# Sharing the 512-column work tiles of the gate and up products between two pools, by pairs

## The chip, the cores and the metric

The kernel runs on one core of one Trainium2 chip. The metric is device time in microseconds of the whole program: the time before is 2663.41 us, the median of 3 runs (2663.13 to 2663.88).

## The reference

One encoder layer on x of shape (1, 2048, 1024): RMSNorm, a projection, windowed attention beside a bidirectional state-space branch, a gated merge with a residual, and then the feed-forward part, which is the one that the change touches:

```python
x = x + (jax.nn.silu(h2 @ w_ffn_gate[layer]) * (h2 @ w_ffn_up[layer])) @ w_ffn_down[layer]
return rmsnorm(x, norm_f_g)
```

Here h2 is the normalised x (2048 x 1024), and the gate and up matrices are 1024 x 2816.

## The kernel before

Three phases follow each other. `phase3` (L1267) ends with the feed-forward part: `gate_up` twice, once for each half of the 2048 tokens, and then `down`. Precision is kept by splitting each operand into a high and a low float32r part (`hi_lo`, L1002: ScalarE copies the high part, VectorE subtracts the low part) and multiplying high*high, high*low and low*high (`PASSES`).

**The unit of work.** A matrix product of 2 x 2 blocks is done with seven block products instead of eight (a Strassen-Winograd scheme; the products are named 11, S2, S1, 12, S3, S4, 22 in `BLK`). `w_unit` (L1034) loads a 1024 x 256 slice of the gate or the up matrix into two raw tiles, forms the sums of its blocks on GpSimd (`sums`, L1021, into a tile T of which there is one) and splits the seven into high and low weights. `h_blocks` (L1006) does the same for the activations of one half of the tokens: 14 tiles H, loaded once for each half. `gu_unit` (L1060) is one unit: seven products of 12 matmuls each, accumulated in three PSUM tiles A, B and C, with the outputs taken out of PSUM between products:

- c1 copies A after product 11 (L1071, ScalarE); u2 = B + c1 after S2 (L1075, VectorE); c5 copies C after S1 (L1079, ScalarE); u3 = B + c1 after S3 (L1086, VectorE); u2 += C after S4 (L1089); c1 += B after 22 (L1095); u3 += c5 (L1093, GpSimd).
- Products accumulate on the same PSUM tile. S3 cannot start on B before u2 has been taken out of it, 22 not before u3, and S4 not on C before c5.

**The pair.** A gate unit and an up unit of the same 256 columns make a pair; 11 pairs make up each half. `pair_up` (L1123) joins them: the gate's four results become Z["11"] (a new tile sg, written by the Silu from PSUM), Z["12"] (u2), Z["22"] (u3) and Z["21"] (c1), and the up unit's results are multiplied into them (L1134). So a gate's c1, u2, u3 and sg live until `z_blocks` (L1098) has read them: it forms two sums zsum and two more in place on GpSimd (L1114 to L1119), splits each of the seven blocks and stores them for `down`. An up unit's c1, u2 and u3 and every c5 live only until they have been added or multiplied in.

**The two pools.** All of these are tiles of 128 x 512 float32 from `t_tile` (L1054): eight buffers in the pool `tq`, six in the pool `tp`. Before the change, the gate's c1, u2, sg and u3 and the up's c1, u2 and u3, seven tiles in a pair, come from the pool of six; the two c5 and the two zsum come from the pool of eight. The first pair of the first half differs (`first`), since the pool of six does not exist yet when it begins: its c1 and u2 are in the pool of eight and its c5 in the pool of six.

**What sets the order.** `gate_up` (L1138) goes through the pairs: gate, weights of the next gate, up, then `z_blocks`; the first and the last pair of a half run their gate and up alternately, product by product (L1145 to L1147). In the first half `h_sums_later` (L991) runs after the second, fourth, sixth and eighth pair: GpSimd makes sums for the second half's activations in the tile T and stores them. After the last pair of the first half the 14 tiles H are filled anew. Each engine executes its instructions in a fixed order. The framework's scheduler writes that order when the kernel is built (`schedule_with_timeline_sim`, L1347), going forward in time through a simulation: an instruction that comes earlier in the program goes first if it is ready, and a new tile gets a buffer when one is free. So with another supply of buffers the order can change from the first affected tile on, and not before it.

Of the kernel before, what the change touches and what calls it, by code (L numbers as in the profile page):

```python
# [86 lines left out]
def rest(gen):  # L87
    for _ in gen:
        pass


class Kern:
# [7 lines left out]
    def load(self, out, in_):  # L100
        self.nc.sync.dma_start(out=out, in_=in_)  # L101
# [955 lines left out]
            return self.tq.tile([128, 512], F32, tag="t", name=name, bufs=8)  # L1057
        return self.tp.tile([128, 512], F32, tag="t", name=name, bufs=6)

    def gu_unit(self, W, H, fin, first=False):  # L1060

        s, v, p = self.s, self.v, self.p
        tl = self.t_tile

        def prod(ps, n, first, last):
            self.chain(ps, [(W[n][:, a, k], H[n][k // 2][:, b, k % 2]) for k in range(4) for a, b in PASSES], first, last)

        A, B, C = self.ps("pj"), self.ps("b"), self.ps("a")
        prod(A, "11", True, False)
        c1 = tl(first, "c1")  # L1070
        s.activation(c1, A, AF.Copy)  # L1071
        yield
        prod(B, "S2", True, False)
        u2 = tl(first, "u2")
        v.tensor_tensor(u2, B, c1, ADD)  # L1075
        yield
        prod(C, "S1", True, False)
        c5 = tl(not first, "c5")
        s.activation(c5, C, AF.Copy)  # L1079
        yield  # L1080
        prod(A, "12", False, True)
        fin("11", A)
        yield
        prod(B, "S3", False, False)
        u3 = tl(False, "u3")
        v.tensor_tensor(u3, B, c1, ADD)  # L1086
        yield
        prod(C, "S4", False, True)
        v.tensor_tensor(u2, C, u2, ADD)  # L1089
        fin("12", u2)  # L1090
        yield
        prod(B, "22", False, True)
        p.tensor_tensor(u3, u3, c5, ADD)  # L1093
        fin("22", u3)
        v.tensor_tensor(c1, B, c1, ADD)  # L1095
        fin("21", c1)
# [23 lines left out]
        put("S3", Z["21"])  # L1120
        put("S4", Z["12"])

    def pair_up(self, W, Wu, H, first=False):  # L1123

        s, v, p = self.s, self.v, self.p
        Z = {}

        def gate(n, z):
            g = self.t_tile(False, "sg") if n == "11" else z
            s.activation(g, z, AF.Silu)  # L1130
            Z[n] = g

        def up(n, z):
            (p if n == "22" else v).tensor_tensor(Z[n], Z[n], z, MULT)  # L1134

        return Z, self.gu_unit(W, H, gate, first), self.gu_unit(Wu, H, up, first)

    def gate_up(self, units, W, hh, H, nxt, bg, after=None, head=None):  # L1138


        n = len(units)
        load = lambda u: self.w_unit(*units[u]) if u < n else nxt()
        for u in range(0, n, 2):
            Z, g, up = head if u == 0 and head else self.pair_up(W, load(u + 1), H)
            if u in (0, n - 2):  # L1145
                Wn = load(u + 2)
                rest(zip_longest(g, up))  # L1147
            else:
                rest(g)
                Wn = load(u + 2)  # L1150
                rest(up)
            if u == n - 2 and after:
                H = after()
            self.z_blocks(hh, u // 2, Z)
            bg(u)
            W = Wn
        return W, H
# [109 lines left out]
    def phase3(self, x, g2, w_glu, w_sb, w_out, wg, wu, wd, gfin, out):  # L1267
        g2 = self.vec_g(g2, "g2")
        self.x2D = self.dram.tile([SEQ, D], F32, name="x2D")
        self.hD = [{n: self.dram.tile([128, 4, 512], F32, name=f"h{hh}{n}") for n in BLK + ("21",)} for hh in range(2)]  # L1270
        self.zD = [[self.dram.tile([4, 128, 7, 2, kc, 128], F32, name=f"z{hh}{c}") for c, (_, kc) in enumerate(CHUNKS)]
                   for hh in range(2)]
        self.hf = {}
        with ExitStack() as es:
            pool = self.pool("p3", 1, es)
            S = self.glu_quarter(pool, w_glu, 0)
            X = None
            for q in range(4):
                M = self.branch_s_quarter(pool, w_sb, S, q)
                if q:  # L1280
                    self.norm_hs(q - 1, X, g2)
                if q < 3:
                    S = self.glu_quarter(pool, w_glu, q + 1)
                X = self.out_quarter(x, w_out, M, q)
        self.mid_es.close()
        self.hi_on_act = True
        self.nw = 0
        self.w2 = self.pool("w2", 1)
        units = [(w, 2 * jp) for jp in range(11) for w in (wg, wu)]
        with ExitStack() as es:  # L1290
            h1 = self.pool("gh", 1, es)
            self.tq = self.pool("tq", 1, es)
            W = self.w_unit(*units[0])
            Wu = self.w_unit(*units[1])
            H = self.h_blocks((h1,), 0, BLK[:3])
            head = self.pair_up(W, Wu, H, True)
            for _ in range(2):
                for g in head[1:]:
                    next(g)
            self.act_es.close()  # L1300
            self.tp = self.pool("gt", 1, es)
            h2 = self.pool("gi", 1, es)
            H.update(self.h_blocks((h1, h2), 0, BLK[3:6]))
            self.norm_hs(3, X, g2)
            self.acb_es.close()
            h3 = self.pool("gj", 1, es)
            pools = h1, h2, h3
            H.update(self.h_blocks(pools, 0, BLK[6:]))
            W, H = self.gate_up(units, W, 0, H, lambda: self.w_unit(*units[0]),
                                lambda u: u in (2, 6, 10, 14) and self.h_sums_later(u // 4),  # L1310
                                lambda: self.h_blocks(pools, 1, BLK), head)
            W, H = self.gate_up(units, W, 1, H, lambda: self.wd_chunk(wd, *CHUNKS[0]), lambda u: None)
        self.dz, self.dw, self.dm, self.dx = (self.pool(n, 1) for n in ("dz", "dw", "dm", "dx"))
        self.down(W, wd, gfin, out)
# [36 lines left out]
```

## Time and profile before

| what | value |
| --- | --- |
| time, median of 3 runs | 2663.41 us |
| the profiled execution | 2669.15 us, of which the span is 2667.4 us |
| PE busy | 2556.7 us (96%) |
| DVE busy | 1931.6 us (72%) |
| POOL busy | 1287.0 us (48%) |
| ACT busy | 1033.7 us (39%) |
| stage of gate and up | 1327 to about 2215 us of the span |

PE is TensorE, DVE VectorE, ACT ScalarE and POOL GpSimd. Times in rows are in us from the span's start. In rows the profile leaves the numbers out of tile names, so c stands for c1 and c5, u for u2 and u3; the line number tells them apart. In a row of the timeline, the number in brackets is how long the engine sat idle before it and what it had been waiting for; "x12" is how many instructions of one kind were merged. In a row of the windows, the columns are length of the stretch, busy time of PE, weight loads, DVE, ACT and POOL with their instruction counts, the granted TensorE clock as a share of full speed, the DMA share and GB/s.

### The profile page before, as it was taken

The page shows a single profiled execution, that of the slowest core. Times are in us where ns is not written, and L with a number is a line of the kernel's source. Part 1 is how long each engine was busy: PE and PEld are TensorE (multiplying, and loading weights), DVE is VectorE, ACT ScalarE, POOL GpSimd, SP SyncE. Part 2 cuts the span into 40 slices and gives each one's busy share as a digit, 9 for nine tenths or more (in the row PEclk, how much of TensorE's full clock was granted, in tenths as well). Part 3 has the DMA queues.
Part 4 walks back from the last instruction along what each step waited for, and adds up shares of the span by engine and source line. Part 5 has one row for each costly group of instructions (what it writes and reads, how often), then busy time and mean ns, then how long its engine had stood idle before and what let it go on. Part 6 is the DMA issues. An engine that isn't in the chain of part 4 may idle for free. (4 is left out here: it accounts for less than half of the span.)

```text
span 2667.4 us, 34485 instructions
## 1 busy us (share of the span) xinstructions
PE 2556.7 (96%) x12090; PEld 2116.3 (79%) x12090; DVE 1931.6 (72%) x2734; ACT 1033.7 (39%) x1878; POOL 1287.0 (48%) x1007
## 2 busy tenths in 40 slices
PE   8999989999999799999988999998999999999998
PEld 7888779888777578887877787776888887887887
DVE  5889477775699847666587678778788777466567
ACT  4322365665223203444453344444344445111113
POOL 2387322331678402234336666746566664364336
PEclk9999999999999899999999999999999999999999
DMA  5346643332555547557566556566455548776547
GB/s 165 102 139 213 186 129 88 86 95 71 181 182 184 154 134 226 193 190 248 162 206 174 174 169 178 166 193 178 135 160 154 154 144 278 256 279 238 222 176 257
DMA packets 451917, 467.94 MB, mean 175 GB/s; under 512 B 82848, under 2 KB 381856, under 8 KB 446624
## 3 DMA queue, kind: packets, MB, share of 16 engines
q1 hardware_dynamic: 451744, 465.75, 55.3%
q8 instruction: 95, 1.56, 0.2%
q14 instruction: 78, 0.64, 0.1%
HBM read 299.99 MB, written 165.68 MB: 175 GB/s over the span
## 5 line engine op out<-in xcount | busy, mean ns | idle before, releaser
L458 PE MATMUL ps_pj<-h,w 128*128 128x512 f32 x1920 | 485.6, 402 | 0.1
L458 PEld LDWEIGHTS ps_pj<-h,w 128*128 128x128 f32 x1920 | 355.3, 188 | 80.7 <-issue 1.5
L1052 PE MATMUL ps_b<-H,w 128*128 128x512 f32 x1584 | 390.3, 397 | 24.3 <-DVE u L1086 14.1
L1052 PEld LDWEIGHTS ps_b<-H,w 128*128 128x128 f32 x1584 | 301.8, 191 | 93.5 <-DVE u L1086 16.7
L1052 PE MATMUL ps_a<-H,w 128*128 128x512 f32 x1056 | 263.7, 394 | 8.2 <-ACT c L1079 6.3
L1052 PE MATMUL ps_pj<-H,w 128*128 128x512 f32 x1056 | 255.3, 390 | 2.5 <-ACT H L1003 2.2
L1004 DVE TENSOR_TENSOR w<-T,w 128x512 fp32r<-128x512 f32 x220 | 210.7, 963 | 64.0 <-ACT w L1003 61.6
L1052 PEld LDWEIGHTS ps_a<-H,w 128*128 128x128 f32 x1056 | 200.8, 190 | 51.5 <-ACT c L1079 6.7
L1052 PEld LDWEIGHTS ps_pj<-H,w 128*128 128x128 f32 x1056 | 197.9, 188 | 44.3 <-ACT H L1003 2.6
L1004 DVE TENSOR_TENSOR w<-raw,w 128x512 fp32r<-128x512 f32 x165 | 201.0, 1219 | 41.0 <-ACT w L1003 40.9
L1003 ACT ACTIVATE w<-T 128x512 fp32r<-128x512 f32 x220 | 135.7, 627 | 231.5 <-POOL T L1024 71.2
L1052 PE MATMUL ps_b<-w,z 128*128 128x512 f32 x792 | 205.6, 395 | 5.6 <-DVE xa L1212 3.4
L424 DVE TENSOR_TENSOR w<-raw,w 128x1024 fp32r<-128x1024 f32 x111 | 157.7, 1422 | 64.7 <-ACT w L421 60.4
L1023 POOL TENSOR_TENSOR T<-raw 128x512 f32<-128x512 f32 x55 | 83.7, 1522 | 244.8 <-DVE w L1004 131.1
L1052 PEld LDWEIGHTS ps_b<-w,z 128*128 128x128 f32 x792 | 150.0, 190 | 39.5 <-DVE xa L1212 5.1
L688 POOL TENSOR_SCALAR P<-P,st 128x384 f32<-128x384 f32 (+1 forms) x128 | 72.8, 588 | 191.6 <-DVE st L686 150.1
L421 ACT ACTIVATE w<-raw 128x1024 fp32r<-128x1024 f32 x93 | 98.0, 1055 | 160.5 <-PE ps_pj L458 65.8
L468 PE MATMUL ps_pj<-w,h 128*128 128x256 f32 x1152 | 154.5, 285 | 3.0 <-DVE V L552 1.3
L468 PEld LDWEIGHTS ps_pj<-w,h 128*128 128x128 f32 x1152 | 142.8, 189 | 6.8 <-DVE V L552 1.9
L1003 ACT ACTIVATE w<-raw 128x512 fp32r<-128x512 f32 x165 | 102.4, 623 | 116.1 <-PE ps_pj L1052 50.6
L1212 DVE TENSOR_TENSOR xa<-xa,ps_b 128x512 f32<-128x512 f32 x128 | 87.3, 685 | 77.8 <-PE ps_b L1052 76.1
L1052 PE MATMUL ps_pj<-w,z 128*128 128x512 f32 x528 | 139.1, 391 | 2.9 <-DMA z<-z 1.6
(333 smaller groups left out, 5098.0 us busy)
## 6 DMA issues: line engine op xcount, KB each, us to landing
z<-zs SPq DMA_DIRECT2D x308, 256.0 KB
z<-z SPq DMA_DIRECT2D x40, 1792.0 KB
raw<-in_w_in SPq DMA_DIRECT2D x52, 512.0 KB
raw<-in_w_ffn_gate SPq DMA_DIRECT2D x44, 512.0 KB
raw<-in_w_ffn_up SPq DMA_DIRECT2D x44, 512.0 KB
x<-in_x SPq DMA_DIRECT2D x32, 512.0 KB
gD<-go SPq DMA_DIRECT2D x32, 512.0 KB
tg<-gD SPq DMA_DIRECT2D x64, 256.0 KB
```

Source lines behind the costliest of these rows:

```text
L421: self.s.activation(hi, src, AF.Copy)
L424: (lo_eng or self.v).tensor_tensor(lo, src, hi.bitcast(F32), SUB)
L458: self.pe.matmul(ps, W[a][:, k, cs], H[k][:, b, sl], start=(i == 0), stop=(i == n - 1))
L468: self.pe.matmul(ps, H[k][:, a, off:off + 128], W[k // 4][b][:, k % 4, :], start=(i == 0), stop=(i == n - 1))
L688: p.tensor_scalar(P[i], P[i], den[:, i:i + 1], 1.0, MULT, MULT)
L1003: self.s.activation(hi, src, AF.Copy)
L1004: self.v.tensor_tensor(lo, src, hi.bitcast(F32), SUB)
L1023: eng.tensor_tensor(T[:, 0], b12, b11, SUB)
L1052: self.pe.matmul(ps, a, b, start=(first and i == 0), stop=(i == n - 1), skip_group_check=True)
L1212: v.tensor_tensor(x[n], x[n], ps, ADD)
```

## The change

The two pools stay as large as they are. Which tile comes from which is new:

- Even pairs (the first, third, ... eleventh of each half): the gate's c1, u2, sg and u3 come from the pool of eight. Odd pairs: all four from the pool of six, as before.
- Every up's u3 comes from the pool of eight; its c1 and u2 stay in the pool of six.
- The c5 and zsum tiles stay in the pool of eight. The first pair of the first half stays as it was.

```diff
-    def gu_unit(self, W, H, fin, first=False):
+    def gu_unit(self, W, H, fin, c1u2, u3_, c5_):
...
-        c1 = tl(first, "c1")
+        c1 = tl(c1u2, "c1")
...
-        u2 = tl(first, "u2")
+        u2 = tl(c1u2, "u2")
...
-        c5 = tl(not first, "c5")
+        c5 = tl(c5_, "c5")
...
-        u3 = tl(False, "u3")
+        u3 = tl(u3_, "u3")
...
-    def pair_up(self, W, Wu, H, first=False):
+    def pair_up(self, W, Wu, H, even, first=False):
...
-            g = self.t_tile(False, "sg") if n == "11" else z
+            g = self.t_tile(even and not first, "sg") if n == "11" else z
...
-        return Z, self.gu_unit(W, H, gate, first), self.gu_unit(Wu, H, up, first)
+        return (Z, self.gu_unit(W, H, gate, even, even and not first, not first),
+                self.gu_unit(Wu, H, up, first, not first, not first))
...
-            Z, g, up = head if u == 0 and head else self.pair_up(W, load(u + 1), H)
+            Z, g, up = head if u == 0 and head else self.pair_up(W, load(u + 1), H, u % 4 == 0)
...
-            head = self.pair_up(W, Wu, H, True)
+            head = self.pair_up(W, Wu, H, True, True)
```

The first argument of `t_tile` chooses the pool of eight when true. In a pair after the first, the pool of six now gives two tiles to an even pair and six to an odd one (seven to each before), and the pool of eight nine and five (four to each before). The last pair of the first half and the first of the second are both even.

## The prediction

> **What bounds the kernel now.** First the page: which engine fills the span, and where that engine waits in the products of gate and up.
>
> ```profile
> PE 2556.7 (96%) x12090; PEld 2116.3 (79%) x12090; DVE 1931.6 (72%) x2734; ACT 1033.7 (39%) x1878; POOL 1287.0 (48%) x1007
> ...
> L1052 PE MATMUL ps_b<-H,w 128*128 128x512 f32 x1584 | 390.3, 397 | 24.3 <-DVE u L1086 14.1
> ```
>
> PE is the bound, so only time in which PE stands still or runs at half clock can be won. The change adds and removes no instruction: it can only move such time. The group row says what to look for: on PSUM tile B, PE was idle for 24.3 us, most of it until u3 (L1086) had been taken out. Next, the stage in windows: the first half after its start, the hand-over from the first half of the tokens to the second, and the second half.
>
> ```profile
> 1400.00:1480.00 80.00, 72.53 (x309) 58.80 (x308) 60.86 (x65) 29.92 (x52) 48.74 (x32) 0.96 0.57 166
> 1480.00:1760.00 280.00, 272.93 (x1192) 224.11 (x1191) 210.71 (x227) 117.49 (x206) 188.28 (x120) 0.99 0.56 168
> 1760.00:1850.00 90.00, 77.06 (x310) 61.23 (x309) 76.66 (x78) 46.13 (x70) 47.17 (x29) 0.92 0.71 208
> 1850.00:2215.00 365.00, 365.00 (x1612) 302.35 (x1611) 291.19 (x304) 161.63 (x279) 233.94 (x145) 1.00 0.53 156
> ```
>
> From 1850 on PE is busy all the time at full clock: nothing can be won there, and a matmul takes 365/1612 = 0.226 us from start to start, so a product of twelve 2.7 us and a pair of 168 matmuls 38 us. The losses lie before 1850. The list of PE's own waits over the stage has these on top, and the timeline of PE shows each.
>
> ```profile
> PE ps_b L1052 <- DVE u L1086: 14.1, 6, 4.6
> PE ps_a L1052 <- ACT c L1079: 6.3, 1, 6.3
> PE ps_b L1052 <- DVE u L1075: 4.9, 4, 1.8
> ```
>
> ```profile
> 1407.15 6.57 PE L1052 MATMUL ps_b<-H,w 128*128 128x512 f32 x19 [4.64 <-DVE u L1086]
> ...
> 1453.37 3.01 PE L1052 MATMUL ps_b<-H,w 128*128 128x512 f32 x12 [2.51 <-DVE u L1086]
> ...
> 1524.41 3.70 PE L1052 MATMUL ps_b<-H,w 128*128 128x512 f32 x15 [1.61 <-DVE u L1075]
> ...
> 1534.14 3.01 PE L1052 MATMUL ps_b<-H,w 128*128 128x512 f32 x12 [1.27 <-DVE u L1086]
> ...
> 1603.58 3.71 PE L1052 MATMUL ps_b<-H,w 128*128 128x512 f32 x15 [1.14 <-DVE u L1075]
> ...
> 1613.31 3.02 PE L1052 MATMUL ps_b<-H,w 128*128 128x512 f32 x12 [1.26 <-DVE u L1086]
> ...
> 1683.39 5.30 PE L1052 MATMUL ps_b<-H,w 128*128 128x512 f32 x15 [1.78 <-DVE u L1075]
> ...
> 1789.48 7.36 PE L1052 MATMUL ps_b<-H,w 128*128 128x512 f32 x24 [2.63 <-DVE u L1086]
> ...
> 1806.09 5.14 PE L1052 MATMUL ps_a<-H,w 128*128 128x512 f32 x12 [6.30 <-ACT c L1079]
> ...
> 1840.23 7.37 PE L1052 MATMUL ps_b<-H,w 128*128 128x512 f32 x24 [1.81 <-DVE u L1086]
> ```
>
> The rows of 1524, 1603 and 1683 stand 79 and 80 us apart, which is two pairs: every second pair stalls, namely the third, fifth, seventh and ninth (even ones in the code's count). They follow the odd pairs, after which GpSimd also makes the sums of `h_sums_later`. The rows of 1789 and 1840 are the last pair of the first half and the first of the second.
>
> A stall also costs clock. The windows over seven stretches in which the granted clock was 0.50 include these:
>
> ```profile
> 1404.51:1411.34 6.83, 4.19 (x10) 3.32 (x11) 4.73 (x7) 3.11 (x6) 4.33 (x3) 0.50 0.87 241
> 1684.40:1687.82 3.42, 3.42 (x9) 2.65 (x8) 1.19 (x3) 2.12 (x4) 3.42 (x3) 0.50 0.85 243
> 1790.22:1793.63 3.41, 3.41 (x9) 2.65 (x9) 2.31 (x3) 2.52 (x3) 3.26 (x2) 0.50 1.04 357
> 1803.87:1810.70 6.83, 4.61 (x11) 3.64 (x12) 6.83 (x4) 4.24 (x7) 6.75 (x5) 0.50 0.76 211
> 1841.42:1844.83 3.41, 3.41 (x10) 2.63 (x9) 1.58 (x2) 1.81 (x4) 2.11 (x2) 0.50 0.55 154
> ```
>
> Half of PE's busy time in such a stretch is lost: 2.1, 1.7, 1.7, 2.3 and 1.7 us. Each begins during or within 1.3 us of the end of a stall above.
>
> The Trainium skill, page "TensorE: Matmul & The Clock Gate", Part 1, says that the clock halves after an idle window of about 3.4 us. Here idle times of 1.78, 2.63 and 1.81 us were followed by half clock and one of 2.51 us (1453.37) was not, so the measurement and the rule differ; by the rule alone the three terms of 1.7 us would not belong to these stalls, and my sum below would be 10.5 instead of 14 us.
>
> **Why the even pairs stall.** The fifth pair's gate, in PE, ScalarE, GpSimd and VectorE rows:
>
> ```profile
> 1504.50 2.43 PE L1052 MATMUL ps_pj<-H,w 128*128 128x512 f32 x10
> ...
> 1510.07 1.29 POOL L1023 TENSOR_TENSOR T<-raw 128x512 f32<-128x512 f32 x1 [7.13 <-DMA raw<-in_w_ffn_gate]
> ...
> 1512.56 1.74 POOL L1093 TENSOR_TENSOR u<-u,c 128x512 f32<-128x512 f32 x1
> ...
> 1515.51 1.29 POOL L1134 TENSOR_TENSOR u<-u,u 128x512 f32<-128x512 f32 x1
> ...
> 1517.68 0.58 ACT L1071 ACTIVATE c<-ps_pj 128x512 f32<-128x512 f32 x1
> ...
> 1521.39 0.68 DVE L1134 TENSOR_TENSOR c<-c,c 128x512 f32<-128x512 f32 x1
> 1521.99 1.77 DVE L1004 TENSOR_TENSOR w<-raw,w 128x512 fp32r<-128x512 f32 x1
> 1523.68 0.68 DVE L1075 TENSOR_TENSOR u<-ps_b,c 128x512 f32<-128x512 f32 x1
> ...
> 1533.41 0.68 DVE L1086 TENSOR_TENSOR u<-ps_b,c 128x512 f32<-128x512 f32 x1
> ```
>
> Product 11 is done at 1506.9, and c1 is copied at 1517.68, almost 11 us later. In between all six buffers are taken: four by the fourth pair's Z, which `z_blocks` has not read yet, one by its up's c1 (until 1521.39 + 0.68), one by its up's u3 (until GpSimd multiplies it in, 1515.51 + 1.29). GpSimd is late because it stood idle 7.13 us before its next sum. c1 comes 0.9 us after the last of these frees a buffer, and u2 after the next, the up's c1, is free at 1522.07. S3 waits for u2, and that is the stall at 1524.41. That c1 and u2 each follow a freed buffer is my reading; no row names a buffer.
>
> **The change part by part.**
>
> *Gates of even pairs to the pool of eight.* When an even pair begins, that pool holds at most two zsum and the up's c5 and u3 of the pair before; the even gate adds c1, u2, c5, sg and u3. That would be nine, but c5 and u3 are gone by 1516.8 (the L1134 row), while the gate's u3 was due only after S3, with its row at 1533.41. So seven are live at most, and c1 and u2 wait for no buffer. What goes: the six idle times of the third to ninth pair, 2.51 + 1.61 + 1.27 + 1.14 + 1.26 + 1.78 = 9.6, and the 1.7 of the half clock after 1683: together 11.3 us. That is one bound; the other is 0 (or below, in the rivals). I take 10.0, nearer to the first: u2 and u3 can still stand behind a VectorE instruction that is running (1.77 at 1521.99), though PE mostly has another product of 2.7 us to do meanwhile. What is late next in these pairs is GpSimd's weight sums: those for the fifth pair's up, begun at 1510.07, have seven products (19 us) of the gate before them.
>
> *Odd pairs' gates in the pool of six.* They find two tiles of the even pair's up there and four free buffers; their up's c1 and u2 then take the two that have come free, six in all. No stall above lies in an odd pair but that at 1407.15. Nothing won, nothing lost: 0.
>
> *The up's u3 to the pool of eight.* At the hand-over, gate and up alternate and no next pair covers them. There the up's u3 waits for the up's u2 to be multiplied in, as these rows show:
>
> ```profile
> 1786.10 0.68 DVE L1089 TENSOR_TENSOR u<-ps_a,u 128x512 f32<-128x512 f32 x1
> 1786.89 0.69 DVE L1134 TENSOR_TENSOR u<-u,u 128x512 f32<-128x512 f32 x1
> ...
> 1788.74 0.68 DVE L1086 TENSOR_TENSOR u<-ps_b,c 128x512 f32<-128x512 f32 x1
> ```
>
> With another pool the chain is cut. Bounds: 0, and the two idle times with their clock, 2.63 + 1.7 + 1.81 + 1.7 = 7.9 us. I take half, 4 us: the activations H, loaded anew, and the weights of the next up arrive when they did, and part of what is won is spent waiting for them.
>
> *Two even pairs in a row at the hand-over.* The last pair's four Z, two zsum, and the next gate's c1, u2 and both c5 make ten tiles for eight buffers. No row shows such a wait; the nearest is that of 6.30 us for c5 at 1806.09 with its 2.3 of clock. The price lies between another such wait, 8.6 us lost, and 8.6 us won, should that stall be due to the late u2 of the same pair. I take 0, since neither bound has a row that is nearer.
>
> *What stays.* Up to the second pair's up nothing differs: the first pair and the second's gate keep their pools, and the scheduler goes forward in time. So the start and the 4.64 us at 1407.15 with its 2.1 stay. The second half after 1850 stays without idle time.
>
> The sum: 10 + 4 + 0 = 14 us. Against the profiled execution, 2667.4 us of span becomes about 2653 (2669.15 in all becomes 2655). The median of the runs, 2663.41, is 5.7 us below the profiled execution; the same 14 us taken off gives **2649.4 us**. A measurement of this kernel can tell about 0.2%, 5.3 us, from no change.
>
> **The rivals.**
>
> *Slower: VectorE's order was the limit, not the buffers.* The second pair found free buffers (the first pair has c1 and u2 in the other pool), and yet has the longest wait for u3:
>
> ```profile
> 1397.00:1407.00 10.00, 5.51 (x25) 4.23 (x23) 10.00 (x8) 2.85 (x5) 7.72 (x5) 0.88 0.71 204
> ```
>
> VectorE was busy for all of those 10 us with 8 instructions, low parts of weights and of Z, and u3 stood behind them. If free buffers let the same backlog form in each of the third, fifth, seventh and ninth pair, each pays 4.64 + 2.1 = 6.7 us: 27 - 11.3 = +15.7, so 2679. It decides from two such pairs on (13.5 against 11.3). Against it: over 1480 to 1760 VectorE is busy 210.71 of 280 us, 75%, not 100%.
>
> The Trainium skill, page "SBUF — State Buffer", "Who interferes with whom", speaks for this rival: a VectorE instruction with two SBUF inputs contends with a GpSimd one that reads SBUF. The trace agrees as far as low parts of one shape take 1.77 us beside GpSimd work, and u2 and u3, which read PSUM, 0.68; by the rule, z sums that start earlier could stretch more low parts by 1.1 us each, and four of those make a stall like that of the second pair.
>
> *No change, by the hand-over.* The ten tiles for eight buffers cost the 8.6 us, the u3 of the hand-over gains nothing, and the even pairs win 11.3: 2.7 us less, 2660.7. The queue of tiles speaks for it; that c5 was late already with a pool to spare speaks against.
>
> *No change, because the change does not reach the stalls.* If c1 at 1517.68 was late by ScalarE's order and not for a buffer, everything stays: 2663.4. Against it: c1 and u2 each come just behind an instruction that frees a buffer.
>
> *Faster than forecast.* All of 11.3 and 7.9, and the c5 stall too (8.6) because u2 comes earlier: 27.8 less, 2635.6; with the clock terms partly kept about 2640.
>
> **How the numbers follow.** Forecast (6 to 19.2 us won, 2644 to 2657) 0.60; faster than that 0.09; no change by the hand-over 0.12; no change because nothing is reached 0.07; slower by VectorE's order 0.12. So faster by over 0.2% is 0.69, within 0.2% 0.19, slower 0.12. The range takes in both cases of no change and most of the faster one: 2639 to 2664; what is left out is the slower case and some of the fastest, 0.16 together.
>
> **What would show it.** Right: no wait for L1075 or L1086 in PE's timeline between 1440 and 1760, c1 within about 2 us of the end of product 11 in even pairs, no half clock near 1684, and the 4.64 us at 1407 still there. In the hand-over, 22 follows S4 without 2.63 and 1.81 us of idle time. Wrong: waits for L1086 of 2 us or more in even pairs with VectorE busy throughout, a wait for L1079 longer than 6.3 us, or idle time of PE after 1850.

## The result and the profile after

The changed kernel takes 2649.09, 2654.06 and 2646.70 us, against 2663.13 to 2663.88 us for the kernel before on the same chip. The ratio is 0.9943, with a 95% interval of 0.9929 to 0.9958: faster by 0.6%. Taking medians, 2663.27 − 2649.09 = 14.2 us were won, where 14 were predicted. One further run of the changed kernel, of 2832.52 us at a mean granted clock of 0.847, is left out of the comparison as disturbed.

The profiled execution after is the one of 2649.09 us, with a span of 2647.3. The span before was 2667.4 us, so these two executions are 20.1 us apart, more than the medians are. Counting the gate and up matmuls in both traces and comparing when each count is reached shows where. The difference was 1.0 us at the start of the stage and 1.7 us at the end of the second pair, where no instruction stands in another order yet. That much is variation between executions. From there to the middle of the eleventh pair it grows to 14.25 us, and by the second pair of the second half to 20.08 us, where it stays. So the pairs won 14.25 − 1.7 = 12.6 us (10 predicted) and the hand-over 5.8 us (4 predicted). Together that is 18.4 us where the medians differ by 14.2: the only trace of the kernel before is of an execution 5.9 us above its median, so some 4 us of the two stages may be that execution's own.

From the page after, the engines' busy times and the group of matmuls on tile B:

```profile
PE 2545.7 (96%) x12090; PEld 2110.9 (80%) x12090; DVE 1920.5 (73%) x2734; ACT 1032.4 (39%) x1878; POOL 1271.4 (48%) x1007
...
L1052 PE MATMUL ps_b<-H,w 128*128 128x512 f32 x1584 | 385.4, 393 | 14.8 <-DVE u L1086 7.4
```

The counts of instructions are those of before. The idle time ahead of tile B's matmuls fell from 24.3 to 14.8 us. The windows of the stage, with the columns as before:

```profile
1400.00:1480.00 80.00, 75.44 (x324) 61.92 (x323) 66.57 (x67) 33.31 (x58) 57.78 (x37) 0.96 0.63 183
1480.00:1760.00 280.00, 279.62 (x1232) 230.76 (x1231) 225.49 (x234) 122.43 (x212) 188.12 (x119) 1.00 0.61 176
1760.00:1850.00 90.00, 79.14 (x335) 63.92 (x334) 74.36 (x81) 46.42 (x74) 52.32 (x33) 0.96 0.67 199
1850.00:2200.00 350.00, 350.00 (x1546) 289.79 (x1544) 266.18 (x295) 152.82 (x264) 220.80 (x140) 1.00 0.56 161
```

From 1480 to 1760 PE is now idle for 0.4 us instead of 7. From 1760 to 1850 the clock is 0.96 instead of 0.92, and 335 matmuls fall in that window instead of 310, in part because the hand-over now comes 14 us earlier. After 1850 nothing has changed. The timeline of PE after, of which these are the rows that had to wait between 1400 and 1850:

```profile
1405.39 4.85 PE L1052 MATMUL ps_b<-H,w 128*128 128x512 f32 x11 [4.56 <-DVE u L1086]
...
1601.37 3.03 PE L1052 MATMUL ps_b<-H,w 128*128 128x512 f32 x12 [0.38 <-DVE u L1086]
...
1767.51 3.06 PE L1052 MATMUL ps_b<-H,w 128*128 128x512 f32 x12 [0.77 <-DVE u L1086]
...
1776.65 3.06 PE L1052 MATMUL ps_b<-H,w 128*128 128x512 f32 x12 [2.69 <-DVE c L1095]
...
1787.49 5.17 PE L1052 MATMUL ps_pj<-H,w 128*128 128x512 f32 x12 [5.75 <-ACT c L1071]
...
1840.82 5.51 PE L1052 MATMUL ps_b<-H,w 128*128 128x512 f32 x23 [1.66 <-DVE u L1086]
```

The six stalls of the third to ninth pair are gone but for 0.38 us. The second pair's is still there (4.56 us, 4.64 before). In the hand-over the waits have changed their names: the 6.30 us for c5 (L1079) has become 5.75 us for c1 (L1071), and in place of 2.63 us for u3 there are 0.77 us for u3 and 2.69 us for B to be added to c1 (L1095).

**A pair's end in both traces.** The cause can be read in the fourth pair, an odd one; the second pair, odd too, has the same picture. VectorE's timeline before, with the up's u2, the product that consumes it, and the up's u3:

```profile
1493.79 0.67 DVE L1075 TENSOR_TENSOR u<-ps_b,c 128x512 f32<-128x512 f32 x1
...
1505.43 0.69 DVE L1134 TENSOR_TENSOR u<-u,u 128x512 f32<-128x512 f32 x1
1506.15 0.69 DVE L1086 TENSOR_TENSOR u<-ps_b,c 128x512 f32<-128x512 f32 x1
```

And the same u2 and u3 in VectorE's timeline after:

```profile
1488.28 0.69 DVE L1075 TENSOR_TENSOR u<-ps_b,c 128x512 f32<-128x512 f32 x1 [0.24 <-PE ps_b L1052]
...
1496.44 0.69 DVE L1086 TENSOR_TENSOR u<-ps_b,c 128x512 f32<-128x512 f32 x1 [0.50 <-PE ps_b L1052]
```

Before, u3 came 12.4 us after u2, right behind the instruction with which u2 is used up. After, it comes 8.2 us later, right behind its matmuls (the bracket names PE). What this does to GpSimd, which has to multiply u3 in twice (L1093, L1134), is seen in its timeline. Before, the last sum of `h_sums_later` and the first of `z_blocks` were at:

```profile
1501.32 1.61 POOL L987 TENSOR_TENSOR T<-hr,T 128x512 f32<-128x512 f32 x1
...
1524.85 1.74 POOL L1114 TENSOR_TENSOR zsum<-c,u 128x512 f32<-128x512 f32 x1
```

Between them lie the rows quoted in the prediction: a weight sum (L1023) first, after 7.13 us of idle time, then L1093 and L1134 among the other sums. GpSimd's timeline after:

```profile
1494.10 1.30 POOL L987 TENSOR_TENSOR T<-hr,T 128x512 f32<-128x512 f32 x1
1497.28 1.29 POOL L1093 TENSOR_TENSOR u<-u,c 128x512 f32<-128x512 f32 x1 [1.88 <-DVE u L1086]
1498.64 1.63 POOL L1134 TENSOR_TENSOR u<-u,u 128x512 f32<-128x512 f32 x1
1501.54 1.28 POOL L1023 TENSOR_TENSOR T<-raw 128x512 f32<-128x512 f32 x1 [1.26 <-DMA h1S<-T]
...
1509.76 1.67 POOL L1114 TENSOR_TENSOR zsum<-c,u 128x512 f32<-128x512 f32 x1 [1.83 <-DVE c L1134]
```

The two steps on u3 now stand ahead of the weight sum, which has its own wait (for the stores of the tile T that it will overwrite), and `z_blocks` begins 15.7 us after L987 instead of 23.5. None of these rows is of the even pair's gate, where the prediction put the gain.

### The profile page after: what moved, and what is told of

Its sections match the earlier page's. It is cut to its first block, busy times and chain, and to the rows that moved or that the text cites. A ratio compares the mean times of both kernels' runs of the same rounds, so it can differ in the third digit from the quotient of the medians.

```text
span 2647.3 us, 34575 instructions
## 1 busy us (share of the span) xinstructions
PE 2545.7 (96%) x12090; PEld 2110.9 (80%) x12090; DVE 1920.5 (73%) x2734; ACT 1032.4 (39%) x1878; POOL 1271.4 (48%) x1007
## 4 chain that ended last, share of the span: by engine, by line
PE 42%; DVE 4%; DMA 4%; POOL 3%; issue 1%; ACT 1%; SPq 0%; DVEq 0%; POOLq 0%; ACTq 0%
PE ps_b L1052 17%; PE ps_a L1052 11%; PE ps_pj L1052 11%; DVE w L1004 2%; PE ps_b L947 1%; PE ps_a L947 1%; DMA z<-z 1%; PE ps_pj L458 1%; DMA hr<-h 1%; DMA hr<-h0S 1%; DMA hr<-h1S 0%; DVE zs L1004 0%; POOL T L1023 0%; POOL T L1025 0%; DVE H L1004 0%
## 5 line engine op out<-in xcount | busy, mean ns | idle before, releaser
L1052 PE MATMUL ps_b<-H,w 128*128 128x512 f32 x1584 | 385.4, 393 | 14.8 <-DVE u L1086 7.4
L1052 PE MATMUL ps_pj<-H,w 128*128 128x512 f32 x1056 | 262.4, 392 | 7.8 <-ACT c L1071 5.8
L1052 PE MATMUL ps_a<-H,w 128*128 128x512 f32 x1056 | 256.7, 391 | 0.0
L1004 DVE TENSOR_TENSOR w<-T,w 128x512 fp32r<-128x512 f32 x220 | 199.0, 909 | 55.6 <-ACT w L1003 53.7
L1003 ACT ACTIVATE w<-T 128x512 fp32r<-128x512 f32 x220 | 136.8, 626 | 202.3 <-POOL T L1024 55.4
L1023 POOL TENSOR_TENSOR T<-raw 128x512 f32<-128x512 f32 x55 | 82.5, 1499 | 152.7 <-DVE w L1004 120.8
L1003 ACT ACTIVATE w<-raw 128x512 fp32r<-128x512 f32 x165 | 103.0, 625 | 123.9 <-PE ps_a L1052 32.9
```

The source lines that it names most:

```text
L1003: self.s.activation(hi, src, AF.Copy)
L1004: self.v.tensor_tensor(lo, src, hi.bitcast(F32), SUB)
L1023: eng.tensor_tensor(T[:, 0], b12, b11, SUB)
L1052: self.pe.matmul(ps, a, b, start=(first and i == 0), stop=(i == n - 1), skip_group_check=True)
```

## The experiments

All of them compute the full result. "Six" and "eight" are the two pools. For each I give how many tiles the pool of six has to give an even and an odd pair (the kernel before 7 and 7, the change 2 and 6). The kernels ran beside the kernel before in four groups; its medians there were 2666.22, 2665.36, 2664.97 and 2664.78 us, so ratios are what to compare. Edits are against the changed kernel unless said otherwise.

**First group: which part, and what set the stalls.** After the result three theories stood. The prediction's: the gates of even pairs bring most of it. A rival: the up's u3 brings it. A second rival, on the trigger: `h_sums_later` decides which pairs stall.

*gates_only* (3 and 7) takes the up's u3 back to the six:

```diff
-                self.gu_unit(Wu, H, up, first, not first, not first))
+                self.gu_unit(Wu, H, up, first, False, not first))
```

> Only the even pairs' gates move to the pool of eight; every up's u3 stays in the pool of six. Buffers theory: the even pairs need no buffer of the pool of six for their gates, so their waits for u2 and u3 (9.6 us idle and 1.7 us of clock between 1440 and 1760) go as they did with the whole change, 11 to 13 us; in the hand-over the up's u3 again waits for the up's u2. Time 2650 to 2654. Rival (the up's u3, which GpSimd frees late, is what mattered): at most 4 us won, 2659 or more.

Measured: 0.9999, interval 0.9990 to 1.0008 (2665.61 us). The part that was to bring 10 us brings nothing by itself, so this expectation failed. PE's waits from 1420 to 1760 (us in total, times, longest):

```profile
PE ps_b L1052 <- DVE u L1086: 8.8, 4, 2.2
```

Before, the same list had 5.1 us for this and 4.5 for L1075. The stalls are now in the fourth, sixth, eighth and tenth pair. They moved on by one pair.

GpSimd's timeline at the fourth pair's end has the two steps on u3 behind the weight sums again, L1093 behind three of them and 11.6 us after L987:

```profile
1498.01 1.30 POOL L987 TENSOR_TENSOR T<-hr,T 128x512 f32<-128x512 f32 x1
1505.37 1.29 POOL L1023 TENSOR_TENSOR T<-raw 128x512 f32<-128x512 f32 x1 [6.05 <-DMA h1S<-T]
...
1509.57 1.74 POOL L1093 TENSOR_TENSOR u<-u,c 128x512 f32<-128x512 f32 x1
```

How GpSimd's delay becomes PE's: the fourth pair's gate runs S3 at nearly the same time in this kernel and in the changed one, so the times can be set side by side. PE, GpSimd and VectorE of *gates_only* in three fences (S3, the third pair's first Z sum, the low parts ahead of the gate's u3, the matmul that waits for it):

```profile
1475.20 2.88 PE L1052 MATMUL ps_b<-H,w 128*128 128x512 f32 x12
...
1486.42 5.55 PE L1052 MATMUL ps_b<-H,w 128*128 128x512 f32 x23 [2.19 <-DVE u L1086]
```

```profile
1473.77 1.29 POOL L1114 TENSOR_TENSOR zsum<-c,u 128x512 f32<-128x512 f32 x1 [5.14 <-DVE c L1134]
```

```profile
1478.92 1.78 DVE L1004 TENSOR_TENSOR w<-raw,w 128x512 fp32r<-128x512 f32 x1
1480.63 1.77 DVE L1004 TENSOR_TENSOR zs<-c,zs 128x512 fp32r<-128x512 f32 x1
1482.32 1.78 DVE L1004 TENSOR_TENSOR w<-raw,w 128x512 fp32r<-128x512 f32 x1
1484.24 1.52 DVE L1004 TENSOR_TENSOR zs<-u,zs 128x512 fp32r<-128x512 f32 x1
1485.69 0.68 DVE L1086 TENSOR_TENSOR u<-ps_b,c 128x512 f32<-128x512 f32 x1
```

The changed kernel's PE, GpSimd and VectorE at the same place:

```profile
1474.93 2.88 PE L1052 MATMUL ps_b<-H,w 128*128 128x512 f32 x12
...
1482.64 5.60 PE L1052 MATMUL ps_b<-H,w 128*128 128x512 f32 x24
```

```profile
1468.66 1.61 POOL L1114 TENSOR_TENSOR zsum<-c,u 128x512 f32<-128x512 f32 x1 [4.53 <-DVE c L1134]
```

```profile
1474.15 1.78 DVE L1004 TENSOR_TENSOR w<-raw,w 128x512 fp32r<-128x512 f32 x1
1475.85 1.78 DVE L1004 TENSOR_TENSOR zs<-c,zs 128x512 fp32r<-128x512 f32 x1
1477.55 1.78 DVE L1004 TENSOR_TENSOR w<-raw,w 128x512 fp32r<-128x512 f32 x1
1479.48 1.55 DVE L1004 TENSOR_TENSOR zs<-u,zs 128x512 fp32r<-128x512 f32 x1 [0.15 <-ACT zs L1003]
1480.96 0.68 DVE L1086 TENSOR_TENSOR u<-ps_b,c 128x512 f32<-128x512 f32 x1
```

The same four low parts stand ahead of u3 in both. But S3 starts 0.3 us apart while the Z sum starts 5.1 us apart and u3 4.7. In the changed kernel u3 is out at 1481.64, one microsecond before PE wants B again at 1482.64; in *gates_only* PE waits 2.19 us. So VectorE's order, the "slower" rival of the prediction, is a real mechanism, and whether it costs anything hangs on how late GpSimd starts the Z. The third pair is even and asks the pool of six for three tiles only; it has the lateness from the second pair, which asks for seven and whose first Z sum (L1114) starts at 1441.31 us in *gates_only* and at 1433.45 in the changed kernel.

*u3_only* (6 and 6) leaves all gates in the six and moves only the up's u3:

```diff
-            g = self.t_tile(even and not first, "sg") if n == "11" else z
+            g = self.t_tile(False, "sg") if n == "11" else z
...
-        return (Z, self.gu_unit(W, H, gate, even, even and not first, not first),
+        return (Z, self.gu_unit(W, H, gate, first, False, not first),
```

> Only every up's u3 moves to the pool of eight; all gates stay in the pool of six. Buffers theory: in an even pair c1 gets the buffer of the up's u2 early, but u2 still waits for the up's c1, so the waits for L1075 and L1086 in the even pairs stay to two thirds or more: 0 to 4 us won there; in the hand-over 22 no longer waits for u3 behind S4, 2 to 6 us won. Time 2654 to 2661. Rival (GpSimd's late freeing of the up's u3 is the whole cause): the even pairs' waits go, 11 to 13 us, 2650 or less.

Measured: 0.9947, interval 0.9934 to 0.9959 (2652.38 us): most of the gain by time, from the part that I had credited with the hand-over only. On VectorE the fourth pair's up has u3 8.2 us after u2 (1491.49 to 1499.65), as in the changed kernel. PE's waits from 1420 to 1760 are not all gone, though:

```profile
PE ps_b L1052 <- DVE u L1086: 6.2, 4, 1.8
```

They went from 9.6 us to about two thirds, as the buffers theory had said, and didn't vanish, as its rival had; the time came out 1.6 us below the range of the first and 2.4 above the bound of the second. How much of it was won in the pairs and how much in the hand-over, the table below tells.

*hsums_later* (7 and 7) is the kernel before with `h_sums_later` one pair later:

```diff
-                                lambda u: u in (2, 6, 10, 14) and self.h_sums_later(u // 4),
+                                lambda u: u in (4, 8, 12, 16) and self.h_sums_later(u // 4 - 1),
```

> The kernel before, with the four sums of h_sums_later one pair later (after the third, fifth, seventh and ninth pair). If GpSimd's extra work is what makes the next pair's buffers late, the waits for u2 and u3 leave the fifth, seventh and ninth pair and stand in the fourth, sixth, eighth and tenth, 8 to 12 us in all; time within 4 us of the kernel before. Rival (the even pairs stall for another reason): the waits stay near 1524, 1603 and 1683 us.

Measured: 0.9992, interval 0.9981 to 1.0002 (2662.12 us). PE's waits from 1420 to 1760:

```profile
PE ps_b L1052 <- DVE u L1075: 7.3, 4, 2.1
PE ps_b L1052 <- DVE u L1086: 2.5, 2, 1.2
```

They sum to 9.8 us (9.6 before) and stand in the fourth, sixth, eighth and tenth pair, as expected. These sums on GpSimd are the trigger that picks the pairs. The second half has no such sums and, with the same seven tiles, no stall: a seventh tile alone isn't enough.

*flip_second_half* (2 and 6) swaps even and odd in the second half, so that no two even pairs meet at the hand-over:

```diff
-            Z, g, up = head if u == 0 and head else self.pair_up(W, load(u + 1), H, u % 4 == 0)
+            Z, g, up = head if u == 0 and head else self.pair_up(W, load(u + 1), H, u % 4 == 2 * hh)
```

> The changed kernel with even and odd exchanged in the second half, so that the last pair of the first half and the first of the second no longer take their gates from the same pool. Buffers theory: the wait of 5.75 us for c1 at the hand-over (ten tiles for eight buffers) goes in most part, 4 to 8 us with its clock, against the changed kernel: about 2642 to 2647. Rival (ScalarE's order and the loading of H hold c1): within 2 us of the changed kernel, 2647 to 2653.

Measured: 0.9923, interval 0.9909 to 0.9936 (2645.26 us). PE's waits from 1760 to 1850 have no c1 any more:

```profile
PE ps_b L1052 <- DVE c L1095: 3.2, 1, 3.2
PE ps_a L1052 <- ACT c L1079: 3.1, 1, 3.1
```

The changed kernel waits 5.8 us for c1 there and 2.7 for L1095. So c1's wait belongs to the two even pairs in a row, and c5's comes back, at half, without them. Whether it is worth time, the third group says.

**Second group: whose u3?** Two theories stood. The order theory: any up's u3 that waits for a buffer comes late and makes the next pair late, so the even pairs' ups stall the odd pairs' gates. The count theory: odd pairs ask the pool of six for seven tiles.

*gates_odd_u3* (3 and 6) moves the up's u3 in odd pairs only, *gates_even_u3* (2 and 7) in even pairs only:

```diff
-                self.gu_unit(Wu, H, up, first, not first, not first))
+                self.gu_unit(Wu, H, up, first, not even, not first))
```

```diff
-                self.gu_unit(Wu, H, up, first, not first, not first))
+                self.gu_unit(Wu, H, up, first, even and not first, not first))
```

> Even pairs' gates from the pool of eight; of the ups' u3 only those of odd pairs. Order theory (an up's u3 that waits for a buffer comes late, and then GpSimd does the next weights' sums before it, which makes the next pair late): the ups of even pairs still wait, so the gates of odd pairs keep the four waits of 2.2 us for u3 that gates_only has; 3 to 7 us slower than the changed kernel. Count theory (odd pairs want seven tiles of six): odd pairs now want six, the four waits go, and the time is within 2 us of the changed kernel.

> Even pairs' gates from the pool of eight; of the ups' u3 only those of even pairs. Order theory: the gates of odd pairs are no longer late, the four waits of 2.2 us go, and the even pairs' gates do not depend on the odd pairs' ups for buffers; within 3 us of the changed kernel. Count theory: odd pairs still want seven tiles of six, the four waits stay, and the kernel is 4 to 9 us slower than the changed one.

Measured: 0.9938 (0.9926 to 0.9950, 2647.46 us) for the odd pairs' u3, and 1.0001 (0.9991 to 1.0011, 2666.15 us) for the even pairs'. The order theory had both the wrong way round. The count theory named both, though the second is 20 us slower than the changed kernel (*after_again*, below) and not 4 to 9. With the even gates in the eight, the odd pairs' u3 makes the difference and the even pairs' none. PE's waits from 1420 to 1760, first of *gates_odd_u3*, then of *gates_even_u3*:

```profile
PE ps_b L1052 <- DVE u L1086: 0.3, 1, 0.3
```

```profile
PE ps_b L1052 <- DVE u L1086: 8.9, 4, 2.2
```

A third theory fits as well, that the odd pairs' up's u3 is the pivot, since GpSimd makes `h_sums_later` there. These two kernels don't part it from the count: in them only an odd pair can want a seventh tile.

*both_u3* (5 and 5) drops the even and odd pairs altogether: every u3 from the eight, every sg and every c1 and u2 after the first pair from the six.

```diff
-            g = self.t_tile(even and not first, "sg") if n == "11" else z
+            g = self.t_tile(False, "sg") if n == "11" else z
...
-        return (Z, self.gu_unit(W, H, gate, even, even and not first, not first),
+        return (Z, self.gu_unit(W, H, gate, first, not first, not first),
```

> No parity: in every pair the gate's u3 and the up's u3 come from the pool of eight, all other gate tiles from the pool of six. The up's u3 is early as in u3_only, and the gate's u2 and sg find a buffer sooner. Order theory: what is left is VectorE's run of low parts ahead of the gate's u3, as in u3_only (four waits of 1.3 to 1.8 us in the even pairs); in the hand-over seven live tiles at most in the pool of eight, so no wait for c1. 0.993 to 0.996 of the kernel before. Count theory: fewer buffers wanted than in u3_only, so those four waits go too, and the time is below the changed kernel's by 2 to 6 us.

Measured: 0.9948, interval 0.9936 to 0.9961 (2651.85 us). Its waits for L1086 from 1420 to 1760 are 5.2 us in four: they stay, as the order theory had said for this kernel. The count theory's guess, that with five tiles they go and the time falls below the changed kernel's, failed; by time five tiles do no better than six here.

*after_again* is the changed kernel once more.

> The changed kernel once more, to be timed on the same chip as the next three. From its first runs: 0.993 to 0.996 of the kernel before, with no wait of PE for u2 or u3 over 0.5 us between 1440 and 1760.

Measured: 0.9932, interval 0.9920 to 0.9944 (2646.56 us). The result repeats.

**Third group: pivot or count?** *odd_u3_only* (7 and 6) parts the two: all gates in the six, the up's u3 moved in odd pairs only. By the pivot theory it gains; by the count it doesn't, as even pairs still want seven.

```diff
-            g = self.t_tile(even and not first, "sg") if n == "11" else z
+            g = self.t_tile(False, "sg") if n == "11" else z
...
-        return (Z, self.gu_unit(W, H, gate, even, even and not first, not first),
-                self.gu_unit(Wu, H, up, first, not first, not first))
+        return (Z, self.gu_unit(W, H, gate, first, False, not first),
+                self.gu_unit(Wu, H, up, first, not even, not first))
```

> One tile only: the up's u3 of odd pairs from the pool of eight, every gate and the even pairs' up's u3 from the pool of six. Theory after eight runs: this tile, late by its buffer in the pairs after which GpSimd makes the second half's sums, starts the whole delay; so GpSimd adds its c5 before the next weights' sums, z_blocks of odd pairs begins about 10 us earlier in the pair, and most of the gain is there: 0.993 to 0.997 of the kernel before, 8 to 17 us. Rival (each tile that leaves the pool of six counts by itself): a third of the gain of u3_only or less, 2661 or more.

Measured: 1.0033, interval 1.0019 to 1.0047 (2674.49 us): slower, by 9.5 us. The pivot theory fell. PE's waits from 1420 to 1760:

```profile
PE ps_b L1052 <- DVE u L1086: 14.0, 4, 4.2
PE ps_b L1052 <- DVE u L1075: 3.0, 3, 1.3
```

That is 17.0 us where before had 9.6, and the mean clock of that stretch is 0.97 where it was 0.99:

```profile
1420.00:1760.00 340.00, 323.00 (x1388) 264.53 (x1388) 260.96 (x266) 138.25 (x239) 217.96 (x139) 0.97 0.56 164
```

Half of a repair is worse than none. Why the waits are so long I did not settle. In the fifth pair S3 and the first Z sum start within 0.12 us of those of *u3_only*, but the four low parts ahead of u3 start at 1521.08 instead of 1518.85, 2.2 us later; what makes them late stays open.

*flip_again* and *after_third* are the swap in the second half and the change, side by side once more.

> Even and odd exchanged in the second half, timed beside the changed kernel on one chip. Buffers theory for the hand-over: 1 to 5 us below the changed kernel, as the wait for c1 (4.3 to 5.8 us) becomes a shorter one for c5 and the wait of 1.7 us at 1840 goes. Rival: the hand-over is bound by the loading of H, within 1 us.

> The changed kernel, to be timed beside the two others: 0.992 to 0.996 of the kernel before.

Measured: 0.9921 (0.9908 to 0.9935, 2646.27 us) and 0.9924 (0.9910 to 0.9937, 2645.61 us). The two can't be told apart, as the rival had it: removing the c1 wait of the hand-over is worth nothing that times show.

**Fourth group: the count with another tile.** *gate_u3_only* (6 and 6) takes the other short-lived tile: every gate's u3 to the eight, every up's u3 back to the six. The up's u3 is not moved at all, and yet no pair wants more than six.

```diff
-            g = self.t_tile(even and not first, "sg") if n == "11" else z
+            g = self.t_tile(False, "sg") if n == "11" else z
...
-        return (Z, self.gu_unit(W, H, gate, even, even and not first, not first),
-                self.gu_unit(Wu, H, up, first, not first, not first))
+        return (Z, self.gu_unit(W, H, gate, first, not first, not first),
+                self.gu_unit(Wu, H, up, first, False, not first))
```

> Every gate's u3 from the pool of eight, everything else, every up's u3 too, from the pool of six: six tiles in each pair, but another tile moved than in u3_only. Count theory (the gain comes when no pair wants a seventh tile of six, whichever tile leaves): the up's u3 is the sixth and comes about 8 us after the up's u2, as in the kernels that gained, and the time is 0.992 to 0.996 of the kernel before. Rival (the up's u3 itself must leave, since it is the tile that GpSimd frees): the up's u3 still comes 12 us after the up's u2, and the time is within 4 us of the kernel before.

Measured: 0.9942, interval 0.9929 to 0.9956 (2651.41 us). This is what the count theory expected. PE's waits from 1420 to 1760 are nearly those of *u3_only*:

```profile
PE ps_b L1052 <- DVE u L1086: 6.1, 4, 2.0
```

All kernels in one table, sorted by whether some pair wants a seventh tile. The "waits" are those of PE for L1075 and L1086 from 1420 to 1760; "u2 to u3" is the time between the two in the fourth pair's up, on VectorE. The last two columns compare each trace with that of the kernel before as in the section on the result, by when PE starts the same count of gate and up matmuls: what was won from the end of the second pair to the middle of the eleventh, and from there to the end of the thirteenth.

| kernel | six: even, odd | ratio | waits, us | u2 to u3, us | won in the pairs, us | in the hand-over, us |
| --- | --- | --- | --- | --- | --- | --- |
| before | 7, 7 | 1 | 9.6 | 12.4 | 0 | 0 |
| hsums_later | 7, 7 | 0.9992 | 9.8 | 11.4 | −1.3 | 2.6 |
| gates_only | 3, 7 | 0.9999 | 8.8 | 12.4 | −3.8 | 5.7 |
| gates_even_u3 | 2, 7 | 1.0001 | 8.9 | 12.4 | −3.7 | 6.0 |
| odd_u3_only | 7, 6 | 1.0033 | 17.0 | 10.7 | −12.0 | 2.8 |
| u3_only | 6, 6 | 0.9947 | 6.2 | 8.2 | 4.7 | 5.2 |
| gate_u3_only | 6, 6 | 0.9942 | 6.1 | 8.2 | 4.5 | 6.6 |
| both_u3 | 5, 5 | 0.9948 | 5.2 | 8.2 | 7.3 | 6.4 |
| gates_odd_u3 | 3, 6 | 0.9938 | 0.3 | 8.2 | 12.7 | 6.8 |
| the change | 2, 6 | 0.9943, 0.9932, 0.9924 | 0.3 to 0.5 | 8.2 | 12.6, 12.5, 12.8 | 5.8, 7.3, 6.9 |
| flip_second_half | 2, 6 | 0.9923, 0.9921 | 0.2 to 0.4 | 8.2 | 12.5, 12.5 | 7.0, 4.7 |

In *odd_u3_only* the seventh tile is in even pairs, so the u3 to look at is the fifth pair's; it comes 12.9 us after its u2.

The last two columns say more than the times. In the pairs, the kernels with at most six tiles win and those with seven lose. The hand-over joins two even pairs (in *flip_second_half* an even and an odd one), and there the gain goes with the even pairs' count: 4.7 to 7.3 us with at most six, 2.8 or less with seven. All entries stand against one trace of the kernel before, and a stretch of half clock more or less moves one by 1.7 us.

## Why the prediction was right, and where it was wrong

The time was right: 14 us forecast, 14.2 measured, and within the range. Of how it came about, half was wrong, and that the sum is so close is luck: neither part is worth its term by itself.

- **"Gates of even pairs to the pool of eight … I take 10.0": failed as a part of its own.** Alone, it loses 3.8 us in the pairs (*gates_only*). In the arrangements run, the pairs gain if, and only if, no pair wants a seventh tile from the pool of six: 4.5 to 12.8 us, by whatever tile they get there. The buffers were rightly named as the limit, but I counted them at the gate that stalled, and the shortage arose one pair earlier, in the up ahead of it. There the seventh tile, the up's u3, waits until u2 is used up; GpSimd's two steps on it fall behind the next weight sums; the Z start about 5 to 8 us later; and the stall appears where u2 or u3 of a later gate has the least time to spare. Giving that gate free buffers only moved the stall to the next pair. That u3 waits for a buffer is my reading, from where it stands and from what moves it; no row names a buffer.
- **"The up's u3 … 4 us", credited with the hand-over only: failed as a division.** The quoted wait of u3 behind u2 was the right observation. I said it matters only where no next pair covers it. It matters in the middle pairs of the first half as well, in odd ones (*gates_even_u3* against the change) and in even ones (*odd_u3_only* against *u3_only*): alone it wins 4.7 us there. And the hand-over doesn't need it: *gates_only* and *gate_u3_only*, which leave every up's u3 in the pool of six, win 5.7 and 6.6 us there.
- **What the even gates do on top.** With at most six in each pair, moving them takes the remaining four waits from 6.2 us to 0.4, and what the pairs win from 4.7 us to 12.6. So this part is worth some 8 us, but only together with the other. By ratios this can hardly be told: 0.9947 without, 0.9924 to 0.9943 with them. The traces show it, 12.5 to 12.8 us in six with the even gates moved against 4.5 to 7.3 in three without.
- **"Odd pairs' gates in the pool of six … 0."** No run moves the odd gates alone, but the odd pairs' ups, with their seventh tile, were where *gates_only* lost what it should have won.
- **c1's lateness was not the cause.** I named as a sign that c1 would follow product 11 within 2 us in even pairs. In the fifth pair after the change, product 11 was done at about 1501.6 and c1 was copied at 1512.00 (ScalarE's L1071), still 10 us late, and PE did not stall. PE runs product 11 well ahead; c1 stands on ScalarE behind the split of the first Z sum, for which ScalarE had been idle for 2.88 us (L1003 at 1511.47, waiting for L1114), and it has that time.
- **The "slower" rival.** Its mechanism, low parts queued on VectorE ahead of u3, occurs in *gates_only* and *odd_u3_only*, and the second is the slower kernel. In the change it is there too, and hidden by 1.0 us in the fourth pair. The 12% were fair for a mechanism so near.
- **The hand-over.** 5.8 us against the 4 forecast. The wait of 2.63 us went, others of 0.77 and 2.69 us came, and the 6.30 us for c5 became 5.75 us for c1. The 1.81 us became 1.66. What was won in the main is clock: before, half clock was granted for 3.41 us from 1790 and from 1841, costing 1.7 us each; after, neither stretch is there, and only the one of 6.83 us beside the long wait stays (from 1785). The price of 0 for ten tiles on eight buffers holds: the c1 wait is theirs (*flip_second_half*), and undoing it changed nothing.
- **"What stays" held**: 4.56 us in the second pair, no idle time after 1850.

Not tried: the direct test of the count, a seventh buffer in the pool of six with the tiles left as they were. Open too: why *odd_u3_only* loses as much as 12 us in the pairs.

## What to carry to other kernels

Count, for each stretch of work, every tile that it asks of a pool, the short-lived ones too, and compare with the pool's buffers: one tile too many can delay not only its own step but all that stands behind it in in-order queues, and the stall may show on another engine a pair later. It need not: the second half of this kernel had the same seven tiles, no extra sums on GpSimd, and no stall. A stall's row tells who was late last, so go back along each queue to the first instruction that moved, and test by moving one tile at a time. Parts of such a change need not add up: here, in the pairs, one part alone lost 3.8 us, the other alone won 4.7, both together won 12.6, and a third version, with one kind of pair mended, lost 0.3% of the whole time. Total times hid this; the same stretch of work compared in each trace showed it.

## What the hardware showed that was not expected

Equal waits were not equally dear. In *gates_only* PE waits 2.19 or 2.22 us for u3 four times, in the fourth, sixth, eighth and tenth pair. The first is quoted above (1486.42, 5.55 us for 23 matmuls); the second:

```profile
1565.82 7.11 PE L1052 MATMUL ps_b<-H,w 128*128 128x512 f32 x23 [2.19 <-DVE u L1086]
```

Its 23 matmuls took 1.6 us longer: a stretch of half clock followed it, as it did the third, and not the first and the last. The Trainium skill, page "TensorE: Matmul & The Clock Gate", Part 1, has the clock halve after an idle window of about 3.4 us; these waits are shorter, and two of four were followed by half clock, so here the measurement decides.

What tells them apart is where they fall. Between 1400 and 2200 us of all fourteen traces, the stretches of half clock stand on a grid of 3.41 us, which lies differently in each trace; in *gates_only* those of the sixth and eighth pair begin at 1567.27 and 1649.19, 24 steps apart. The windows of four such steps of *gates_only*, two with the first wait, one with the second, and the one after it:

```profile
1481.94:1485.35 3.41, 2.29 (x11) 1.56 (x9) 3.26 (x3) 0.73 (x2) 3.33 (x3) 1.00 0.91 248
1485.35:1488.76 3.41, 2.34 (x10) 1.93 (x11) 3.41 (x5) 1.17 (x3) 3.25 (x2) 1.00 0.80 211
...
1563.86:1567.27 3.41, 1.45 (x6) 1.23 (x7) 3.41 (x4) 1.15 (x2) 3.33 (x3) 1.00 0.85 205
1567.27:1570.68 3.41, 3.41 (x9) 2.65 (x9) 2.23 (x4) 2.66 (x5) 0.72 (x1) 0.50 0.70 225
```

The first wait is cut by the end of a step, so that PE was idle for 1.12 us of one and 1.07 of the next, and the clock stayed full. Of the second, 1.96 us lie in one step, and the next had half clock. In these traces every step at full clock of which PE was idle for 1.88 us or more was followed by half clock, none with less than 1.77 us was, and between the two both occur. So a stall of some 2 us costs 1.7 us more or nothing, by where it falls on the grid, and its price can be forecast only to within that.

The runs of the kernel before, which lay within 0.8 us on the first chip (its profiled execution of 2669.15 us aside), spread from 2657.22 to 2672.11 us on the others, so that parts of a change were better compared by stage than by one run's time.
